# One more FFN piece at the mixer boundary, and a new schedule of weight casts, in a decoder layer on eight cores

## The chip, the cores and the metric

The kernel runs one decoder layer on 8 cores of one Trainium2 chip. The metric is device time in microseconds (us) of the slowest core. Cores 0 to 3 are one die, 4 to 7 the other.

Two programs share the work. The *first program* (cores 0 and 4) takes the first 4608 tokens of each of the two sequences: nine tiles of 512, of which the first two are worked as a pair. The *halo program* (cores 1, 2, 3, 5, 6, 7) takes 3928 tokens. Because its attention looks back 2048 tokens, it first works four tiles of halo in two pairs (the *pair stage*, roughly the first 680 us) and then eight own tiles.

Runs come in two states. In the slow state the cores of a die are granted a lower TensorE clock, and the time is longer by some per cent to 20%. Even among fast runs there is a step: in some of them cores 2 and 3 alone are granted 0.989 instead of about 0.998 and take some 30 us more.

## The reference, cut to what matters

```python
h = x + 0.5 * post1(SwiGLU1(pre1(x)))          # FFN1, 1024 -> 2816 -> 1024
u = pre_mix(h)                                 # then q/k/v projections, three attentions, a gated merge
h = h + post_mix(merged @ w_out)
y = h + 0.5 * post2(SwiGLU2(pre2(h)))          # FFN2
# pre*, post*, pre_mix, post_mix are RMS norms; 32768 tokens in all, D_MODEL 1024, D_FF 2816
```

The kernel's matmuls take bf16 weights, while the inputs are float32, so each core casts weights as it goes.

## The kernel before: the parts that matter

**Pieces.** The first half of an FFN (`x @ w_in`, SwiGLU) is cut into 22 pieces of 16 matmuls, one piece of weights each. While one tile is in its attention and its boundaries, pieces of the *next* tile's FFN1 are slipped in by `fill(1)`, so that TensorE has something to do:

```python
def fill(n):                     # F[0] is the generator of the next tile's FFN1 pieces
    for _ in range(n):
        if F[0] is None: return
        try: next(F[0])
        except StopIteration: F[0] = None
```

**Boundaries.** Between FFN1 and the mixer, and between the mixer and FFN2, a tile of 512 tokens is normalised and transposed block by block. TensorE transposes into PSUM; VectorE evicts into `xn`, times the gain (1.22 us for 128x1024 on core 2); only then can the next matmuls read `xn`. The end of this is `tail`. `gain` is 1 (G_MIX) at the mixer boundary, 2 (G_F2) before FFN2. The pair edges of the pair stage inherit `tail` with gain 1.

```python
def tail(self, more=lambda: fill(1)):
    fin_pool[0] = FIN4
    z = self.nb - 1
    more()
    self.scaled(z - 1)           # ScalarE: h * rstd of the last block but one
    self.stat(z)
    more()
    self.scaled(z)
    self.turn(z - 1)             # TensorE transposes, VectorE evicts to xn
    self.turn(z)
    more()
```

The order of each engine is fixed at build time by a list scheduler.

**Weights.** Eleven slots in SBUF hold weight pieces. A piece comes into a slot in one of two ways: by a cast from the float32 input (`wslot<-wf`, issued on POOL), or by a plain load from a bf16 copy in HBM (`wslot<-wsc`, issued on SP). The copy is made in one of two ways: by a *store* of a slot after some use (`wsc<-wslot`), or by an *ahead cast* in HBM, before any use (`wsc<-wf`):

```python
def release(k):                  # after a use of a piece
    ...
    if nm not in W["stored"] and n == stored_at(role, nm) and n + 1 < uses[nm]:
        W["stored"].add(nm)
        dma("sp", wsc[...], slots[s]..., ...)      # store: bf16 slot -> copy
def w_ahead(nm, gate=()):
    ...
    dma("pool", wsc[...], wf[...], ...)            # ahead cast: float32 -> bf16 copy
```

In the halo program before, the ahead casts are issued in the second half of the pair stage, one every two FFN pieces; the FFN2 pieces that are not cast ahead are stored at their first use (even numbers) or their second (odd ones):

```python
SECOND = ["f2_i%d" % f for f in range(9, NF, 2)]                    # stored at second use
LATE = [n for n in PT if n.startswith("f2_o")] + ["f2_i%d" % f for f in range(8)]   # 20 pieces
...
            while F[0] is not None:
                fill(1)
                step(prep)                 # row loads and squares of the next tile
                n += 1
                if n % 2 == 0 and late:
                    w_ahead(late.pop(0))
```

The softmax here doesn't subtract the row's maximum and nothing guards it: scores larger than these inputs give would overflow.

## Time and profile before

Six runs: 3479.99, 3509.78, 3511.83, 3695.24, 3801.16 and 3926.94 us, median 3603.54. The last three are slow. The profiled run was fast, with cores from 3465.0 to 3479.3 us at a granted clock of 0.996 to 0.998. Core 2 was the slowest.

The page of core 2, parts 1 and 4 (busy us per engine with the share of the span; then the chain of work that ended last, by engine):

```profile
PE 3430.2 (99%) x19230; PEld 1743.1 (50%) x19230; DVE 1690.0 (49%) x2656; ACT 955.8 (27%) x1685; POOL 853.0 (25%) x1161
...
PE 96%; DMA 2%; DVE 1%; ACT 1%; issue 1%; POOL 0%; SPq 0%; POOLq 0%; ACTq 0%; DVEq 0%
```

TensorE is the bound. What a change of order can win is TensorE's idle time, and the list of waits gives it. Its main lines for core 2 (what waited, for what: us in total, times, longest us):

```profile
PE ps L586 <- DMA wslot<-wsc: 9.0, 3, 4.0
PE ps L586 <- DVE xn L621: 6.7, 7, 1.6
PE ps L1582 <- DVE ident_sb L618: 5.8, 1, 5.8
PE ps L774 <- DVE q L631: 4.9, 4, 2.1
...
PE ps L586 <- ACT V L616: 3.1, 2, 2.3
```

All lines together come to 41.6 us, 1.2% of the span. The first line is the wait for weights and the second the wait for an evicted `xn`; the next two belong to start-up.

The wait for weights is at 480 to 490 us in the pair stage, in the second half of FFN1. The view of windows on core 2 shows the DMA engines full before it (columns: window, its length, busy us of PE, PEld, DVE, ACT, POOL with instruction counts, granted clock, DMA share, GB/s):

```profile
400.00:440.00 40.00, 40.00 (x187) 18.13 (x186) 16.50 (x24) 6.66 (x12) 5.85 (x12) 1.00 0.99 160
440.00:470.00 30.00, 30.00 (x141) 13.58 (x140) 6.56 (x6) 0.00 (x0) 1.46 (x3) 1.00 1.02 196
470.00:480.00 10.00, 7.58 (x36) 3.33 (x35) 5.88 (x7) 1.85 (x5) 3.88 (x2) 1.00 0.99 168
480.00:490.00 10.00, 3.42 (x13) 1.00 (x11) 2.10 (x4) 3.28 (x12) 7.38 (x6) 0.79 0.86 240
490.00:500.00 10.00, 10.00 (x41) 4.21 (x40) 0.00 (x0) 0.00 (x0) 0.00 (x0) 0.87 0.06 25
```

TensorE is busy 3.42 of 10 us. Cores 3, 6 and 7 show 7.3 to 7.6 us of the same wait, cores 1 and 5 none.

The wait for `xn` is the mixer boundary. The timeline of core 2's TensorE at one of them (start us, us, engine line op out<-in, count, and in brackets the idle time before it and who ended it):

```profile
1815.54 2.54 PE L586 MATMUL ps<-xn,wslot 128*128 128x512 bf16 x11
1817.91 0.61 PE L774 MATMUL ps<-ident_sb,mix 128*128 128x128 bf16 x8
1818.36 1.24 PE L586 MATMUL ps<-xn,wslot 128*128 128x512 bf16 x5
1820.31 1.89 PE L586 MATMUL ps<-xn,wslot 128*128 128x512 bf16 x8 [0.71 <-DVE xn L621]
```

The last transposes end, five matmuls of an FFN piece are left, and then the projections wait 0.71 us for the eviction. The boundary before FFN2 of the same core has no such wait, because there 20 matmuls of FFN1 pieces stand between the last transposes and FFN2 (the last line runs from them into FFN2 without a break):

```profile
2024.16 2.75 PE L586 MATMUL ps<-xn,wslot 128*128 128x512 bf16 x12
2026.75 0.61 PE L774 MATMUL ps<-ident_sb,mix 128*128 128x128 bf16 x8
2027.20 18.08 PE L586 MATMUL ps<-xn,wslot 128*128 128x512 bf16 x83
```

### The profile page before, as it was taken

To read this page: it belongs to the slowest core of one execution; us is meant where nothing else is said; L and a number is where in the kernel's file an instruction comes from. 1 tells how busy PE (TensorE), PEld (TensorE's weight loads), DVE (VectorE), ACT (ScalarE), POOL (GpSimd) and SP (SyncE) were. 2 spreads that over 40 slices of the span, in tenths; PEclk is the share of its full clock that TensorE was granted. 3 is DMA by queue.
4 is the path that set the end of the run, shared out by engine and by line. 5 is a ranking of instruction groups with operands and counts; after the bars stand their busy time and mean duration, and the time that the engine had idled before them with its cause. 6 is when DMAs were issued, how large, how long until landed. Compare 5 with 4: busy or idle time off the path is not lost.

```text
span 3479.3 us, 54875 instructions; the slowest of 8 cores (3465.0 to 3479.3 us)
## 1 busy us (share of the span) xinstructions
PE 3430.2 (99%) x19230; PEld 1743.1 (50%) x19230; DVE 1690.0 (49%) x2656; ACT 955.8 (27%) x1685; POOL 853.0 (25%) x1161
## 2 busy tenths in 40 slices
PE   8999989999999999999999999999999999999999
PEld 4445445454445544554445444554455444646555
DVE  4444334573437444564347343744456433736533
ACT  2223222232313331233122231333123312333321
POOL 3143122233214230413023211412040302323020
PEclk9999999999999999999999999999999999999999
DMA  9979967657878786668564456445463556446456
GB/s 205 200 159 219 169 127 242 151 129 156 186 238 217 135 213 189 226 151 239 171 221 131 148 177 211 159 131 181 153 222 124 168 161 218 149 150 216 144 170 207
DMA packets 177859, 623.20 MB, mean 179 GB/s; under 512 B 20288, under 2 KB 20928, under 8 KB 177584
## 3 DMA queue, kind: packets, MB, share of 16 engines
q1 hardware_dynamic: 128384, 452.09, 40.4%
q0 software_dynamic: 49200, 167.52, 25.4%
q8 instruction: 163, 2.67, 0.3%
q14 instruction: 112, 0.92, 0.1%
HBM read 659.13 MB, written 69.75 MB: 209 GB/s over the span
## 4 chain that ended last, share of the span: by engine, by line
PE 96%; DMA 2%; DVE 1%; ACT 1%; issue 1%; POOL 0%; SPq 0%; POOLq 0%; ACTq 0%; DVEq 0%
PE ps L586 94%; DMA wslot<-wsc 1%; PE ps L774 1%; DMA wslot<-wf 1%; PE ps L1265 1%; ACT mix L609 0%; DVE xn L621 0%; DMA h<-xh 0%; DVE mix L621 0%; POOL rstd L621 0%; DVE tsig L626 0%; DVE mix L995 0%; ACT tsig L609 0%; ACT q L609 0%; POOL rstd L631 0%
## 5 line engine op out<-in xcount | busy, mean ns | idle before, releaser
L586 PE MATMUL ps<-xn,wslot 128*128 128x512 bf16 (+3 forms) x9840 | 2139.4, 370 | 11.8 <-DVE xn L621 6.7
L586 PEld LDWEIGHTS ps<-xn,wslot 128*128 128x128 bf16 x9840 | 947.6, 98 | 1012.4 <-issue 21.2
L626 DVE SCALAR_TENSOR_TENSOR tsig<-tsig,ps 128x512 f32<-128x512 f32 (+1 forms) x418 | 279.1, 668 | 561.2 <-ACT tsig L609 558.9
L609 ACT ACTIVATE tsig<-ps 128x512 f32<-128x512 f32 (+1 forms) x418 | 242.8, 581 | 847.8 <-PE ps L586 846.5
L586 PE MATMUL ps<-wslot,hid 128*128 128x512 bf16 (+1 forms) x1892 | 413.3, 379 | 0.0
L586 PE MATMUL ps<-wslot,mix 128*128 128x512 bf16 (+1 forms) x1540 | 338.5, 381 | 9.0 <-DMA wslot<-wsc 9.0
L609 ACT ACTIVATE mix<-ps 128x512 bf16<-128x512 f32 (+4 forms) x334 | 210.1, 664 | 447.0 <-PE ps L586 446.0
L621 DVE TENSOR_TENSOR ps<-ps,gpost_sb 128x1024 f32<-128x1024 f32 (+1 forms) x110 | 125.7, 1144 | 401.9 <-ACT mix L609 225.2
L586 PEld LDWEIGHTS ps<-wslot,hid 128*128 128x128 bf16 (+1 forms) x1892 | 185.7, 98 | 220.7 <-issue 0.2
L626 DVE SCALAR_TENSOR_TENSOR mix<-mix,ps 128x512 f32<-128x512 f32 (+1 forms) x192 | 127.9, 666 | 321.8 <-PE ps L586 320.6
L621 POOL TENSOR_TENSOR q<-mix 128x512 bf16<-128x512 f32 (+1 forms) x144 | 216.5, 1504 | 187.2 <-DVE mix L995 115.3
L586 PEld LDWEIGHTS ps<-wslot,mix 128*128 128x128 bf16 (+1 forms) x1540 | 151.5, 99 | 191.4 <-issue 13.6
L609 ACT ACTIVATE mix<-ps,bgate_sb 128x512 f32<-128x512 f32 (+1 forms) x192 | 128.6, 670 | 331.1 <-PE ps L586 331.1
L995 DVE TENSOR_TENSOR mix<-ps,cst 64x512 f32<-64x512 f32 (+1 forms) x308 | 205.7, 668 | 20.6 <-DVE mix L995 0.9
L621 POOL TENSOR_TENSOR mix<-mix 128x512 f32<-128x512 f32 (+1 forms) x64 | 78.0, 1218 | 514.6 <-DVE mix L626 514.6
L621 DVE TENSOR_TENSOR hid<-tsig,ps 128x512 bf16<-128x512 f32 (+1 forms) x242 | 162.1, 670 | 85.0 <-PE ps L586 76.3
L641 POOL DMA_DIRECT2D wslot<-wf x144 | 79.9, 555 | 473.6 <-PE ps L586 291.9
L586 PE MATMUL ps<-mix,wslot 128*128 128x512 bf16 (+1 forms) x640 | 163.9, 370 | 0.0
L586 PE MATMUL ps<-wslot,xn 128*128 128x256 bf16 (+1 forms) x1200 | 155.1, 274 | 3.8 <-ACT V L616 2.3
L621 DVE TENSOR_TENSOR mix<-tsig,ps 128x512 bf16<-128x512 f32 (+1 forms) x176 | 117.2, 666 | 82.5 <-PE ps L586 80.8
L631 POOL TENSOR_SCALAR rstd<-ssq 128x1 f32<-128x1 f32 x178 | 42.1, 236 | 442.6 <-ACT mix L609 246.4
L586 PEld LDWEIGHTS ps<-wslot,xn 128*128 128x128 bf16 (+1 forms) x1200 | 126.5, 110 | 39.1 <-issue 5.4
(159 smaller groups left out, 2424.5 us busy)
## 6 DMA issues: line engine op xcount, KB each, us to landing
wslot<-wsc SPq DMA_DIRECT2D x688, 512.0 KB, 4.8
wslot<-wf POOLq DMA_DIRECT2D x118, 512.0 KB, 10.4
wsc<-wslot SPq DMA_DIRECT2D x71, 512.0 KB, 10.7
wslot<-wsc SPq DMA_DIRECT2D x40, 576.0 KB, 3.7
xs<-xh POOLq DMA_DIRECT2D x41, 512.0 KB, 7.5
h<-xh POOLq DMA_DIRECT2D x32, 512.0 KB, 9.5
y<-h POOLq DMA_DIRECT2D x28, 512.0 KB, 8.1
wslot<-wf POOLq DMA_DIRECT2D x24, 576.0 KB, 7.0
```

Of the source, the lines that this page charges most:

```text
L586: P.add("pe", lambda e: e.matmul(outV.ap, lhsT=lhsV.ap, rhs=rhsV.ap, start=start, stop=stop, skip_group_check=True), reads=[lhsV, rhsV], w ...
L609: return e.activation(out=outV.ap, in_=inV.ap, func=func, scale=scale.ap if isinstance(scale, View) else scale, **kw)
L621: P.add(eng, lambda e: e.tensor_tensor(out=outV.ap, in0=aV.ap, in1=bV.ap, op=op), reads=[aV, bV], writes=[outV], us=0.567 if op == ALU.pow ...
L626: P.add("dve", lambda e: e.scalar_tensor_tensor(out=outV.ap, in0=aV.ap, scalar=sc, in1=bV.ap, op0=op0, op1=op1), reads=[aV, bV] + ([scalar ...
L631: P.add(eng, lambda e: e.tensor_scalar(out=outV.ap, in0=aV.ap, scalar1=sc, scalar2=None, op0=op0), reads=[aV] + ([s1] if isinstance(s1, Vi ...
L641: P.add(eng, lambda e: e.dma_start(out=out, in_=in_), reads=reads, writes=writes, dma_key=key, nbytes=n)
L774: P.add("pe", lambda e, src=src, o_=o_: e.transpose(out=o_.ap, in_=src.ap, identity=ident.ap), reads=[src, ident.v(0, 128)], writes=[o_], ...
L995: P.add("dve", lambda e, a=a, z=z: e.tensor_tensor(out=t2.ap[a:a + 64, :], in0=p_.ap[z:z + 64, :], in1=cst.ap[z:z + 64, TT:TT + n], op=ALU ...
L1265: P.add("pe", lambda e, src=src, o_=o_: e.transpose(out=o_.ap, in_=src.ap, identity=ident.ap[0:n, 0:n]), reads=[src, ident.v(0, 128)], wri ...
```

## The change

The intent, in its author's words: "Same 18 casts, one every three steps; one more piece of the next tile's FFN between FFN1's last transposes and the mixer's projections."

```diff
+TAIL = {1: 2, 2: 1}
 def stored_at(role, nm):
+    if role and nm in THIRD:
+        return 2
     if nm in HELD[role] or role and nm in SECOND:
         return 1
-SECOND = ["f2_i%d" % f for f in range(9, NF, 2)]
+SECOND = ["f2_i%d" % f for f in range(6, NF, 2)]
+THIRD = ["f2_i%d" % f for f in range(7, NF, 2)]
-LATE = [n for n in PT if n.startswith("f2_o")] + ["f2_i%d" % f for f in range(8)]
+LATE_EVERY, LATE_FROM = 3, 31
+LATE = [n for n in PT if n.startswith("f2_o")] + ["f2_i%d" % f for f in range(6)]
 ...                                     # end of Boundary.tail
-                more()
+                for _ in range(TAIL[self.gain]):
+                    more()
 ...                                     # halo program, pair stage
+            def fill_late(k):
+                for _ in range(k):
+                    fill(1)
+                    n[0] += 1
+                    if n[0] >= LATE_FROM and n[0] % LATE_EVERY == 0 and late:
+                        w_ahead(late.pop(0))
-                n += 1
-                if n % 2 == 0 and late:
-                    w_ahead(late.pop(0))
```

So there are three changes in one: an extra piece at every boundary with gain 1; another number and pace of ahead casts; and stores of FFN2 pieces put off by one use. The order of the built programs corrects the words. Before, 20 LATE casts are issued in the pair stage; after, only 14, since the steps end before the list does. Direct casts into slots rise by 23 in the halo program (118 to 141 of 512 KB on core 2) and not at all in the first (213 on core 4). At the first of the two pair edges the extra step is four pieces, since `tail` is called there with `fill(4)`.

More of the change, by code (lines that the diff above doesn't have):

```diff
@@ L1626, in trace @@
             memory_prep()
-            fill(6)
+            n = [0]
+            def fill_late(k):
[4 more added lines that the diff above has]
+                        w_ahead(late.pop(0))
+            fill_late(6)
             memory_turn(xn2)
             for _ in memory(xn2):
-                fill(6)
+                fill_late(6)
             prep = prep_iter(4)
-            n = 0
             while F[0] is not None:
-                fill(1)
+                fill_late(1)
                 step(prep)
-                n += 1
-                if n % 2 == 0 and late:
-                    w_ahead(late.pop(0))
             drain(prep)
```

## The prediction

> **What bounds it now.** TensorE: PE is busy 3430 of 3479 us (99%, profile page) and is 96% of the chain of waits. The list of waits gives core 2's TensorE about 42 us of idle time, so removing waits can win 1.2% at most:
> - Weights in the halo cores' pair stage, 480 to 490 us: 9.0 us on core 2, 7 to 8 on cores 3, 6, 7, none on 1 and 5. The DMA row is full from 280 to 475 us; the 20 ahead-of-use casts there take 28 us each to land (view of DMA issues).
> - Mixer boundary: the projections wait for the eviction of the last transposes (xn by DVE, 1.22 us): 6.7 us in 7 waits on core 2, 7.6 to 7.9 on cores 0 and 4.
> - Start-up, about 18 us: untouched.
> - Pair stage at 268 to 272 and 543 us: 2.4 and 2.3 us.
>
> **What the change does.** The matmul work is equal.
>
> 1. One FFN piece (16 matmuls, 3.45 us) moves to the mixer boundary. In the built order the matmuls between last transposes and projections go from 12 or 13 to 28 or 29, which covers the eviction: -6 to -8 us per core. But a tile has 22 pieces. Before, the 22nd covered the same eviction before FFN2: the run after the last FFN2-boundary transposes falls from 372 to 356, of which 352 are FFN2 itself, so cover drops from 20 matmuls (4.3 us) to 4 (0.86 us). In the timeline those transposes end at 2027.2 us, the eviction runs 2027.47 to 2028.69, FFN2 could start about 2028.9, and PE would run dry at 2028.1. A new wait of about 0.85 us in 5 or 6 tiles: +4 to +5 us. Net -1 to -3 us: the wait moves rather than vanishes.
>
> 2. Casts. The words say "same 18"; in the built order I count 14 ahead casts in the halo program's pair stage instead of 20. Six fewer transfers of 1 MB read and 0.5 MB written in the saturated stretch should remove the 7 to 9 us weight wait on cores 2, 3, 6, 7. The cost comes later: 23 more direct casts, mostly in FFN2 of the first own tiles, 20 in a row in the first (now 14), 16 in the second (now 7), where the DMA row is already at 1.0. Core 4 runs 22 per FFN2 with almost no cast waits, so I expect 0 to 5 us. [...]
>
> 3. The pair edge gets one more step: part of the 2.3 and 2.4 us may go.
>
> **Prediction.** Cores 2, 3, 6, 7: -5 to -12 us; the others -3 to +2. The slowest core ends near 3472 us in a fast profile (3479 before). Three of six runs before were slow (to 3927), fast ones 3480 to 3512; a median over mixed runs can lie far higher, so my figure is 3485 us, range 3455 to 3610. Faster by over 2%: 2%; within 2%: 96%; slower: 2%.
>
> **Right or wrong shows as.** Projections' waits for xn gone, 5 or 6 new ones before FFN2; the weight wait near 480 us gone; ahead casts landing under 28 us; waits for direct casts at 900 to 980 and 1280 to 1350 us under 5 us.
>
> **What would make it wrong.** Direct casts starving FFN2 in the first own tiles (10 us or more); another share of slow runs.

## The result, and the profile after

A ratio is the mean time of one kernel's fast runs over that of the other's fast runs of the same rounds, so it is not quite the ratio of the medians quoted. It is 0.9976, 95% interval 0.9953 to 0.9999: the same within 2%, faster by about a quarter of a per cent. The medians over all runs, slow ones included, were 3476.49 us after (20 runs) and 3509.0 us before (now 40 runs). The low fast times of before lie at 3479 to 3484 us, those of after at 3473 to 3477 us.

In the profiled run (fast) the spans of cores 0 to 7 are 3473.1, 3461.2, 3463.3, 3462.1, 3473.4, 3466.9, 3464.5 and 3461.4 us. The halo cores gained; cores 0 and 4 did not (3470.5 and 3472.3 before) and are now the slowest. The page of core 4, parts 1 and 4, looks like that of before and tells nothing of this:

```profile
PE 3413.2 (98%) x18896; PEld 1697.9 (49%) x18896; DVE 1662.0 (48%) x2608; ACT 956.2 (28%) x1636; POOL 881.5 (25%) x1164
...
PE 96%; DVE 1%; issue 1%; ACT 1%; DMA 1%; POOL 0%; DVEq 0%; ACTq 0%; POOLq 0%; SPq 0%
```

The list of waits of core 2 does (the lines of the kernel are shifted by 7 or 8; L593 is the old L586, L628 the old L621):

```profile
PE ps L1590 <- issue: 6.8, 1, 6.8
PE ps L593 <- DVE xn L628: 6.7, 8, 1.2
PE ps L781 <- DVE q L638: 4.7, 4, 2.1
PE ps L593 <- ACT V L623: 3.6, 2, 2.7
...
PE ps L593 <- DMA wslot<-wsc: 0.2, 1, 0.2
```

The wait for weights is gone, 9.0 to 0.2 us. The wait for `xn` has not moved at all in its sum: 6.7 us before, 6.7 us after. The windows of core 2 show the DMA engines done before the weights are needed, and no fall of the clock:

```profile
400.00:440.00 40.00, 40.00 (x187) 18.08 (x185) 15.89 (x24) 6.57 (x11) 3.70 (x7) 1.00 1.00 173
440.00:470.00 30.00, 30.00 (x140) 13.59 (x139) 8.79 (x8) 0.00 (x0) 0.00 (x0) 1.00 0.71 195
470.00:480.00 10.00, 10.00 (x48) 4.53 (x47) 4.88 (x8) 5.02 (x16) 5.02 (x5) 1.00 0.33 107
480.00:490.00 10.00, 10.00 (x48) 4.56 (x47) 4.04 (x6) 3.09 (x7) 7.33 (x10) 1.00 0.00 0
490.00:500.00 10.00, 10.00 (x60) 5.01 (x58) 6.33 (x8) 6.11 (x11) 3.30 (x8) 1.00 0.00 1
```

The timeline of core 2 shows where the `xn` wait went. At the mixer boundary 29 matmuls now follow the last transposes without a break: the five of before, the 16 of the extra piece and the first eight of the projections. Nothing waits:

```profile
1802.60 2.54 PE L593 MATMUL ps<-xn,wslot 128*128 128x512 bf16 x11
1805.10 0.61 PE L781 MATMUL ps<-ident_sb,mix 128*128 128x128 bf16 x8
1805.54 6.42 PE L593 MATMUL ps<-xn,wslot 128*128 128x512 bf16 x29
1811.80 0.38 PE L593 MATMUL ps<-wslot,xn 128*128 128x256 bf16 x2
```

Before FFN2 only four are left, and FFN2 waits 0.73 us:

```profile
2014.51 2.75 PE L593 MATMUL ps<-xn,wslot 128*128 128x512 bf16 x12
2017.10 0.61 PE L781 MATMUL ps<-ident_sb,mix 128*128 128x128 bf16 x8
2017.55 1.03 PE L593 MATMUL ps<-xn,wslot 128*128 128x512 bf16 x4
2019.30 26.06 PE L593 MATMUL ps<-xn,wslot 128*128 128x512 bf16 x120 [0.73 <-DVE xn L628]
```

### The profile page after: what moved, and what is told of

The parts are those of the page before. It is cut to its first block, busy times and chain, and to the rows that moved or that the text cites. A ratio compares the mean times of both kernels' runs of the same rounds, so it can differ in the third digit from the quotient of the medians.

```text
span 3473.4 us, 53905 instructions; the slowest of 8 cores (3461.2 to 3473.4 us)
## 1 busy us (share of the span) xinstructions
PE 3413.2 (98%) x18896; PEld 1697.9 (49%) x18896; DVE 1662.0 (48%) x2608; ACT 956.2 (28%) x1636; POOL 881.5 (25%) x1164
## 4 chain that ended last, share of the span: by engine, by line
PE 96%; DVE 1%; issue 1%; ACT 1%; DMA 1%; POOL 0%; DVEq 0%; ACTq 0%; POOLq 0%; SPq 0%
PE ps L593 94%; PE ps L781 1%; ACT mix L616 1%; PE ps L1273 1%; DMA wslot<-wsc 1%; DVE mix L628 0%; DVE xn L628 0%; DVE mix L1003 0%; DVE tsig L633 0%; DMA wslot<-wf 0%; PE ps L1590 0%; POOL rstd L628 0%; DVEq L361 0%; ACT q L616 0%; DVE ps L628 0%
## 5 line engine op out<-in xcount | busy, mean ns | idle before, releaser
L593 PE MATMUL ps<-xn,wslot 128*128 128x512 bf16 (+1 forms) x9776 | 2198.5, 377 | 12.0 <-DVE xn L628 6.6
L593 PEld LDWEIGHTS ps<-xn,wslot 128*128 128x128 bf16 x9776 | 942.0, 98 | 1078.7 <-issue 27.1
L633 DVE SCALAR_TENSOR_TENSOR tsig<-tsig,ps 128x512 f32<-128x512 f32 x374 | 256.8, 687 | 550.1 <-ACT tsig L616 549.1
L616 ACT ACTIVATE tsig<-ps 128x512 f32<-128x512 f32 x374 | 222.9, 596 | 829.4 <-PE ps L593 829.4
L616 ACT ACTIVATE mix<-ps 128x512 bf16<-128x512 f32 (+1 forms) x356 | 228.2, 676 | 496.2 <-PE ps L593 491.8
L593 PE MATMUL ps<-wslot,mix 128*128 128x512 bf16 x1584 | 348.1, 380 | 2.6 <-DMA wslot<-wsc 2.6
L593 PE MATMUL ps<-wslot,hid 128*128 128x512 bf16 x1584 | 345.3, 379 | 0.0
L628 DVE TENSOR_TENSOR ps<-ps,gpost_sb 128x1024 f32<-128x1024 f32 (+1 forms) x109 | 128.6, 1182 | 438.1 <-ACT mix L616 253.7
L628 POOL TENSOR_TENSOR q<-mix 128x512 bf16<-128x512 f32 x162 | 252.5, 1560 | 225.1 <-DVE mix L1003 141.4
L628 POOL TENSOR_TENSOR mix<-mix 128x512 f32<-128x512 f32 x72 | 90.9, 1263 | 632.2 <-DVE mix L633 632.2
L593 PEld LDWEIGHTS ps<-wslot,mix 128*128 128x128 bf16 x1584 | 154.9, 98 | 188.9 <-issue 6.0
L593 PEld LDWEIGHTS ps<-wslot,hid 128*128 128x128 bf16 x1584 | 154.7, 98 | 186.0 <-issue 0.7
L1003 DVE TENSOR_TENSOR mix<-ps,cst 64x512 f32<-64x512 f32 x324 | 223.1, 689 | 21.7 <-DVE mix L1003 0.9
L593 PE MATMUL ps<-mix,wslot 128*128 128x512 bf16 x720 | 190.7, 379 | 0.0
L628 DVE TENSOR_TENSOR hid<-tsig,ps 128x512 bf16<-128x512 f32 x198 | 135.6, 685 | 69.2 <-PE ps L593 63.1
L593 PE MATMUL ps<-wslot,xn 128*128 128x256 bf16 x1184 | 154.7, 275 | 3.4 <-DVE hid L633 2.4
L628 DVE TENSOR_TENSOR mix<-tsig,ps 128x512 bf16<-128x512 f32 x176 | 120.9, 687 | 73.1 <-PE ps L593 69.6
L593 PEld LDWEIGHTS ps<-wslot,xn 128*128 128x128 bf16 x1184 | 123.2, 106 | 41.7 <-issue 5.0
```

The source lines that it names most:

```text
L593: P.add("pe", lambda e: e.matmul(outV.ap, lhsT=lhsV.ap, rhs=rhsV.ap, start=start, stop=stop, skip_group_check=True), reads=[lhsV, rhsV], w ...
L616: return e.activation(out=outV.ap, in_=inV.ap, func=func, scale=scale.ap if isinstance(scale, View) else scale, **kw)
L628: P.add(eng, lambda e: e.tensor_tensor(out=outV.ap, in0=aV.ap, in1=bV.ap, op=op), reads=[aV, bV], writes=[outV], us=0.567 if op == ALU.pow ...
L633: P.add("dve", lambda e: e.scalar_tensor_tensor(out=outV.ap, in0=aV.ap, scalar=sc, in1=bV.ap, op0=op0, op1=op1), reads=[aV, bV] + ([scalar ...
L1003: P.add("dve", lambda e, a=a, z=z: e.tensor_tensor(out=t2.ap[a:a + 64, :], in0=p_.ap[z:z + 64, :], in1=cst.ap[z:z + 64, TT:TT + n], op=ALU ...
```

## The experiments

All kernels gave correct results. The table collects the median span of each core over the fast runs, in us. The runs were made on three chips, each time with the kernel before beside them. That kernel's own medians on cores 2, 3, 6 and 7 differ by up to 5.5 us, so between rows of the table only larger differences count. Because the chip times mix in the step of cores 2 and 3, I judge by these spans and by the traces.

| kernel | fast runs | cores 0, 4 | cores 1, 5 | cores 2, 3, 6, 7 |
|---|---|---|---|---|
| before | 5 | 3472.9, 3474.8 | 3464.9, 3462.5 | 3476.9, 3473.5, 3475.9, 3477.3 |
| after (first result) | 18 | 3472.9, 3473.0 | 3461.2, 3461.9 | 3465.3, 3462.0, 3464.1, 3462.6 |
| after_again | 3 | 3474.2, 3469.3 | 3462.5, 3463.2 | 3464.6, 3463.2, 3462.6, 3464.3 |
| casts_only | 6 | 3473.1, 3474.2 | 3470.6, 3471.1 | 3475.8, 3469.8, 3473.7, 3473.1 |
| piece_only | 4 | 3473.6, 3470.5 | 3464.1, 3461.9 | 3478.1, 3478.1, 3477.0, 3475.5 |
| both_covered | 5 | 3471.3, 3470.7 | 3454.5, 3453.2 | 3458.3, 3455.5, 3456.4, 3456.0 |
| pair_edge_only | 5 | 3475.4, 3474.9 | 3463.5, 3463.8 | 3463.7, 3462.6, 3466.1, 3463.9 |
| tiles_only | 2 | 3474.1, 3471.9 | 3469.3, 3470.7 | 3473.5, 3468.1, 3473.4, 3470.9 |
| both_tiles | 4 | 3470.3, 3471.2 | 3454.7, 3455.1 | 3457.4, 3454.8, 3457.9, 3453.9 |
| casts14_every2 | 5 | 3473.1, 3471.7 | 3459.9, 3462.8 | 3463.1, 3463.2, 3462.9, 3463.4 |
| casts_prep_later | 4 | 3473.1, 3472.2 | 3467.4, 3467.4 | 3486.3, 3483.0, 3468.2, 3471.4 |
| early20 | 4 | 3473.6, 3474.4 | 3461.4, 3460.9 | 3471.1, 3466.8, 3472.0, 3472.7 |
| fewer_old_pace | 3 | 3473.8, 3472.6 | 3471.1, 3472.7 | 3484.5, 3478.5, 3484.3, 3483.7 |
| both_tiles_4600 | 4 | 3464.2, 3465.9 | 3457.9, 3453.9 | 3457.5, 3454.8, 3456.2, 3455.2 |
| casts_prep_latest | 4 | 3472.1, 3476.1 | 3463.8, 3461.3 | 3462.9, 3462.1, 3463.9, 3461.7 |
| stores_as_before | 6 | 3472.3, 3474.9 | 3464.6, 3463.8 | 3473.9, 3468.7, 3474.1, 3473.4 |

### The yardstick: the changed kernel again

> The changed kernel once more, as the yardstick of this chip. Both theories: ratio 0.998 to the kernel before; slowest core near 3474 us and of the first program (cores 0 and 4); cores 2, 3, 6, 7 at 3461 to 3466 us.

It repeated: ratio 0.9988, interval 0.9966 to 1.0009, from only three fast runs at 3475.8 to 3476.1 us. Halo cores and first program stood where they were.

### The two halves apart

casts_only is the changed kernel with the extra piece taken out (its 14 casts become 15, since the pair stage has more steps left):

```diff
-TAIL = {1: 2, 2: 1}
+TAIL = {1: 1, 2: 1}
```

> The changed casts, without the extra piece at the mixer boundary. Theory A (the casts give the whole gain, the piece only moves a wait): cores 2, 3, 6, 7 fall from 3468-3479 to 3461-3468 us, the weight wait near 480 us is under 1 us, cores 0 and 4 stay at 3470-3474 us, projections still wait about 7 us for xn; chip time within 2 us of the changed kernel. Theory B (the piece gives the gain): under 3 us of gain on the halo cores, chip time near 3480 us.

The wait for weights near 480 us was gone on all halo cores, as theory A has it. But the halo cores came to 3470 to 3476 us, not to 3461 to 3468, and cores 1 and 5 even lost 6 to 9 us. Theory A failed here: the casts alone do not give the gain. The timeline of core 2 shows a new wait, at a pair edge near 550 us:

```profile
551.16 3.57 PE L593 MATMUL ps<-xn,wslot 128*128 128x512 bf16 x8 [3.67 <-DVE xn L628]
```

After the wait of 3.67 us these 8 matmuls took 3.57 us, where 8 take 1.89 us elsewhere, so the gap costs once more after it has ended (the granted clock was 0.68 between 550 and 560 us). All six halo cores have such a wait here, 3.5 to 5.5 us, also cores 1 and 5, which had no wait for weights to lose; in the kernel before none has it.

piece_only is the kernel before with the extra piece:

```diff
-                more()
+                for _ in range(TAIL[self.gain]):
+                    more()          # TAIL = {1: 2, 2: 1}
```

> The extra piece alone, with the old casts. Theory A: TensorE's total wait for xn is unchanged within 1.5 us (6.7 us on core 2), but stands before FFN2 instead of before the projections; cores 0 and 4 within 2 us of before; cores 2, 3, 6, 7 keep 5 us or more of weight wait near 480 us, chip time 3475 to 3481 us. Theory B: the xn wait falls below 2 us and every core gains 5 us or more.

As theory A: the weight wait stayed (8.8 us on core 2 between 470 and 495 us), cores 2, 3, 6 and 7 did not gain (3475.5 to 3478.1 us), and cores 0 and 4 moved by +0.7 and -4.3 us, within what they move between runs of one kernel. The wait for `xn` on core 2, from the list of waits:

```profile
PE ps L588 <- DMA wslot<-wsc: 9.1, 4, 3.7
PE ps L588 <- DVE xn L623: 6.7, 9, 1.2
```

6.7 us once more. So neither half alone gives the 12 us of the changed kernel on cores 2, 3, 6 and 7. The two act together.

### Where they act together: the pair edges

The extra piece goes to two kinds of place: the pair edges of the pair stage, and the mixer boundaries of the later tiles. pair_edge_only and tiles_only keep the changed casts and give it to one kind each:

```diff
-                for _ in range(TAIL[self.gain]):
+                for _ in range(2 if isinstance(self, PairEdge) else 1):                 # pair_edge_only
+                for _ in range(1 if isinstance(self, PairEdge) else TAIL[self.gain]):   # tiles_only
```

> The changed casts, with the extra step only at the pair edges of the first stage, none at the mixer boundaries of later tiles. Theory A2 (the casts give the gain of the halo cores only together with the extra step at the pair edge, which keeps TensorE fed while ScalarE stands before a late row load; the extra pieces of the later tiles only move a wait): cores 1, 2, 3, 5, 6, 7 at 3461 to 3467 us, no wait of 2 us or more for xn near 550 us, projections still waiting 0.7 to 1.6 us per tile. Rival B2 (the pieces of the later tiles are what halo cores gained over the casts alone): halo cores stay at 3469 to 3476 us. Both: cores 0 and 4 at 3469 to 3475 us.

> The changed casts, with the extra piece only at the mixer boundaries of later tiles, none at the pair edges. Theory A2: like the casts alone, halo cores 3469 to 3476 us with a wait of about 3.7 us for xn near 550 us on core 2. Rival B2: halo cores at 3461 to 3467 us.

Theory A2 holds on both. With the piece at the pair edges alone the halo cores are at 3462.6 to 3466.1 us, as in the changed kernel; with it in the later tiles alone they are at 3468.1 to 3473.5 us, as with the casts alone (only two fast runs, so no ratio, but the trace agrees: core 2 waits 5.46 us for `xn` at 551.79 us). The extra pieces in the later tiles, which the change's words put first, give nothing. (The ratio of pair_edge_only is 0.9985, interval 0.9971 to 0.9998.)

Why does the pair edge need it? In casts_only TensorE reaches this edge some 10 us sooner (its last transposes start at 542.98 us on core 2, against 553.98 us in the kernel before), and there the loads of the next tile's rows (`xs<-xh`) are under way with everything else: the DMA share was 0.96 to 1.00 between 530 and 550 us. In casts_only ScalarE stands 6.76 us at a square of those rows, with two of the FFN's activations (`tsig`) behind it in its list, and runs these only after the square, from 546.48 us (timeline of core 2's ScalarE):

```profile
538.06 0.60 ACT L616 ACTIVATE tsig<-ps 128x512 f32<-128x512 f32 x1 [2.91 <-PE ps L593]
545.42 1.06 ACT L616 ACTIVATE q<-xs 128x1024 bf16<-128x1024 f32 x1 [6.76 <-DMA xs<-xh]
...
546.48 1.06 ACT L616 ACTIVATE tsig<-ps 128x512 f32<-128x512 f32 x2
```

In the trace VectorE then does the late `tsig` and only after it the eviction to `xn` (548.56 us) that TensorE waits for. To test this, casts_prep_later and casts_prep_latest leave the edge without an extra piece and only start the row loads later after the second pair edge:

```diff
                 prep = prep_iter(i + 1)
+                fill(5)                  # casts_prep_later; fill(10) in casts_prep_latest
                 while F[0] is not None:
                     fill(1)
                     step(prep)
+                    step(prep)           # casts_prep_latest only
```

> The changed casts without any extra piece; only the next tile's row loads and their squares begin five FFN pieces later after the second pair edge. Theory A2 (what keeps the casts alone from giving the gain is that ScalarE, in order, stands before a row load that DMA has not landed, and the activations behind it hold up the eviction that TensorE waits for): the wait of 3.7 us for xn near 550 us on core 2 falls under 1 us, halo cores go from 3469-3476 to 3464-3469 us. If instead the extra FFN work at the edge itself is needed: the wait stays at 3 us or more and the halo cores stay at 3469-3476 us.

This was inconclusive. Cores 1, 5, 6 and 7 gained 1.7 to 5.5 us on casts_only, less than expected on most; cores 2 and 3 stood in their low-clock step in two of the four fast runs and say nothing. In the trace core 6 had 0.56 us of `xn` wait near 540 us, but core 7 still 1.98 us for `xn` and 2.46 us for `tsig`, and core 2, of which under 1 us was expected, 1.86 us for `xn`. The reason to go on was that one square still stood behind a single activation.

> As casts_prep_later, with the row loads ten FFN pieces later, so that the first square that waits for a row load stands behind three activations of the FFN instead of one. If a row load in front of the FFN's activations is what eats the casts' gain: on cores 2, 3, 5, 6, 7 less than 1.5 us of waits for xn and tsig between 530 and 570 us, halo cores 3462 to 3467 us in the undisturbed runs. If delay of the loads does not matter beyond what casts_prep_later gave: 3467 to 3471 us.

This one settled it. The halo cores are at 3461.3 to 3463.9 us without any extra piece, like the changed kernel. (With a ratio of 0.9966, interval 0.987 to 1.0061, the chip time alone says nothing.) It has 15 ahead casts, as casts_only has, so it was not the one cast more that held casts_only back. It also changes only what follows the second pair edge, so the first one did not hold it back either. On core 2 there is only one wait of this kind left, 0.46 us for `tsig` at 563 us. ScalarE's list has three activations in front of the first square, and the row has nearly landed when it gets there:

```profile
540.26 0.60 ACT L616 ACTIVATE tsig<-ps 128x512 f32<-128x512 f32 x1 [3.75 <-PE ps L593]
541.47 1.06 ACT L616 ACTIVATE q<-xs 128x1024 bf16<-128x1024 f32 x1 [0.61 <-DMA xs<-xh]
```

In the changed kernel the square waits as well, but two activations stand in front of it, not one, and TensorE has 40 matmuls, the last eight of them projections, to do after the transposes (core 2):

```profile
537.17 0.60 ACT L616 ACTIVATE tsig<-ps 128x512 f32<-128x512 f32 x1 [1.22 <-PE ps L593]
541.65 1.06 ACT L616 ACTIVATE q<-xs 128x1024 bf16<-128x1024 f32 x1 [3.89 <-DMA xs<-xh]
539.53 8.80 PE L593 MATMUL ps<-xn,wslot 128*128 128x512 bf16 x40
```

So the extra piece gives TensorE work at the pair edge and shifts the order of ScalarE's list. Moving the loads does the second alone, and that is enough.

### Number of casts or pace of casts

casts14_every2 is the changed kernel with the same 14 casts at the old pace; early20 has all 20 at the new pace, beginning earlier:

```diff
-LATE_EVERY, LATE_FROM = 3, 31
+LATE_EVERY, LATE_FROM = 2, 31      # casts14_every2, with LATE cut to f2_o and f2_i0, f2_i1
+LATE_EVERY, LATE_FROM = 3, 13      # early20, with LATE to f2_i7
```

> The changed kernel with the same 14 casts ahead, but one every two steps as before, not every three. If the number of casts is what ended the weight wait near 480 us: wait under 1 us, halo cores within 2 us of the changed kernel. If the slower pace is what ended it: 5 us or more of the wait return on cores 2, 3, 6, 7 and they stand at 3466 us or more.

> The changed kernel with 20 casts ahead, one every three steps, but from step 15 on instead of 33. If the number of casts before the DMA queue has to be empty is what counts: the weight wait near 480 us is back at 3 us or more on some of cores 2, 3, 6, 7, since the last cast is issued at the same step as in the changed kernel and the stretch was full before. If only the pace counts: no wait.

At the old pace with 14 casts there is no wait for weights on any halo core in this stretch, and the halo cores are at 3459.9 to 3463.4 us (ratio 0.9981, interval 0.9967 to 0.9995). With 20 casts at the new pace the wait is back, 4.2, 3.6, 7.9 and 9.8 us on cores 2, 3, 6 and 7. The line of core 7:

```profile
PE ps L593 <- DMA wslot<-wsc: 9.8, 3, 3.9
```

The number counts. The pace was hardly put to the test, because the casts did not come out at it: on core 2 the ahead casts of the changed kernel were issued from 315.3 to 412.9 us and those of casts14_every2 from 315.5 to 414.5, with POOL waiting for earlier ahead casts to land (30.8 and 36.7 us in all). With 20 casts the last was issued at 451.0 us before and still at 448.6 us in early20, which began at 291.7 us. The stretch was full before the first cast (in the kernel before, the DMA share of core 2 was 1.00 between 270 and 290 us, with the first cast at 308.6 us), and with the earlier start the last cast was issued only 2.4 us earlier.

### What six fewer ahead casts cost later

fewer_old_pace is the kernel before with nothing but a shorter list:

```diff
-LATE = [...] + ["f2_i%d" % f for f in range(8)]
+LATE = [...] + ["f2_i%d" % f for f in range(2)]
```

> The kernel before with nothing changed but the list of ahead casts cut from 20 to 14 (the other six are cast at their first use). If the number of casts causes the weight wait: wait near 480 us under 1 us on cores 2, 3, 6, 7; by A2 the halo cores gain only part of it, 3466 to 3476 us, as in the run with the changed casts alone.

The wait near 480 us was gone, but the kernel became slower: ratio 1.0025, interval 1.0006 to 1.0044, halo cores at 3471 to 3485 us, where I had expected 3466 to 3476. Part of this is the wait for `xn` at the second pair edge, as in casts_only: 1.3 to 5.7 us on the halo cores. On cores 1 and 5 it is the larger part, 5.7 and 5.4 us, against 1.0 and 2.2 us of waits for loads later. The later cost came where I had looked for it in the prediction, in FFN2 of the first own tile, but not in direct casts: in weight *loads*. On core 6, waits between 900 and 1060 us:

```profile
PE ps L586 <- DMA wslot<-wsc: 12.0, 2, 9.4
```

Neither the kernel before nor the changed one has any wait for DMA there. The changed one differs in that its stores are put off. stores_as_before is the changed kernel with the old rule for the stores:

```diff
-SECOND = ["f2_i%d" % f for f in range(6, NF, 2)]
-THIRD = ["f2_i%d" % f for f in range(7, NF, 2)]
+SECOND = ["f2_i%d" % f for f in range(9, NF, 2)]
+THIRD = []
```

> The changed kernel, but the FFN2 pieces are stored as before (even ones and the six no longer cast ahead at first use, odd ones from 9 on at second use). If the put-off stores are what kept the later cost of the change small: 5 us or more of weight waits between 900 and 1000 us, as in fewer_old_pace (12 us on core 6), halo cores 3468 to 3478 us. If they do not matter: waits under 1 us there and halo cores at 3461 to 3466 us.

The waits are back, 5.5, 4.8, 5.2 and 3.6 us on cores 2, 3, 6 and 7 in the same window, and these cores stand at 3468.7 to 3474.1 us, nearly where they were before the change. On core 2:

```profile
PE ps L593 <- DMA wslot<-wsc: 5.5, 2, 3.1
```

The waits of SP, which issues loads and stores from one list, fit this: on core 6 between 880 and 1060 us it stood 21.8 us for stores in fewer_old_pace and 15.8 us in stores_as_before, with 13 and 12 stores issued there; in the kernel before and in the changed one it stood for none, with ten and four. So putting off the stores is a needed third part: it keeps the stores out of the tile that has just received the casts.

### Giving both boundaries a spare piece

If the piece only moves a wait because a tile has 22 pieces and both boundaries want a spare one, a piece from elsewhere should end both waits. both_covered takes the one between the two heads of mixer A; both_tiles does so except in the two paired tiles of cores 0 and 4:

```diff
-TAIL = {1: 2, 2: 1}
+TAIL = {1: 2, 2: 2}
             attn_a(i, 0, 4)
-            fill(1)
+            if paired:               # both_tiles; no fill at all in both_covered
+                fill(1)
             attn_a(i, 1, 4)
```

> The changed kernel, with the piece taken from between the two heads of mixer A, so that both the mixer boundary and the FFN2 boundary have one left over. Theory A (a tile has 22 pieces and both boundaries need a spare): the xn wait falls from about 6.7 to under 2.5 us on every core, unless the attention opens a new wait of the same size where the piece was; cores 0 and 4 near 3469 us, chip time 3468 to 3472 us. Theory C (the xn wait is not a matter of spare pieces): xn wait stays at 5 us or more and the time stays at 3474-3477 us.

The wait for `xn` fell from 6.7 to 1.4 us on core 2 and from 6.6 to 2.6 us on core 4, and the attention opened no new wait of that size. The halo cores ended 6.5 to 9 us earlier than in the changed kernel. The chip gained less than I had expected of cores 0 and 4: these lost part of it in their paired tiles, where waits of 3.31 us (2.44 before) and a new one of 1.52 us appeared on core 4 at 556 and 602 us. Ratio 0.9979, interval 0.9963 to 0.9995.

> As the run both_covered, but in the first two (paired) tiles of cores 0 and 4 the piece between the heads stays where it was, since those tiles have no mixer boundary to cover and lost about 2.4 us there. Expected if a spare at both boundaries is what is missing: xn waits under 2.5 us, halo cores at 3453 to 3459 us as before, cores 0 and 4 at 3467 to 3471 us, chip time 3468 to 3472 us, 1 to 2 us below both_covered. If start-up noise of cores 0 and 4 decides instead: no change against 3472 to 3474 us.

Those two waits are as before the change again. Ratio 0.9969, interval 0.9954 to 0.9984, cores 0 and 4 at 3470.3 and 3471.2 us. On core 4 no wait for `xn` is left after 700 us (4.1 us in the changed kernel), but the same core waited 6.9 us for weights there in this run against 2.6 us in the changed kernel's. So cores 0 and 4 gained about 2 us by the medians, which is less than core 4 of the kernel before moves (6 us), and end at the upper edge of what I expected. Whether the wait for weights is set by the order or is noise I did not test.

### The bound of the chip time

Cores 0 and 4 are the slowest in the changed kernel. Sixteen tokens too many are handed out over both sequences (4608 + 3 x 3928 = 16392, for 16384 each). both_tiles_4600 takes the eight of each sequence from the first program:

```diff
-FIRST = 4608
+FIRST = 4600
-    yd = nc.dram_tensor("y", [FIRST, D], ...)
+    yd = nc.dram_tensor("y", [-(-FIRST // 128) * 128, D], ...)
```

> As both_tiles, and the first program takes 4600 tokens instead of 4608 (the eight doubly computed tokens dropped), since its cores 0 and 4 are now the slowest. Its last tile is 504 wide instead of 512, 1.6% of about 250 us of matmuls with the tokens as moving side: cores 0 and 4 lose 3 to 5 us, to 3465-3468 us, the others unchanged at 3453-3461 us, chip time 3466 to 3470 us. If cores 0 and 4 do not bound the chip time, it stays at 3472 us.

The 3 to 5 us, and the 250 us in them, were an estimate; in the trace of the changed kernel the 128x512 matmuls of core 4 that read `xn` are busy for 236.4 us between 3100 and 3480 us. That their time goes with their width is near what the kernel before shows on core 2: its 8608 of 128x512 are busy for 1959.5 us, 0.228 us each, and its 1040 of 128x344 for 163.9 us, 0.158 us each.

Cores 0 and 4 fell by 5 to 6 us on both_tiles, the others stayed within 3.2 us of it, and the chip time fell with cores 0 and 4: fast runs at 3466.95 to 3469.4 us, against 3469.9 to 3473.1 us of both_tiles. Ratio 0.9967, interval 0.9952 to 0.9983. But against the kernel before beside them their ratios are nearly equal (0.9969 and 0.9967), so how much of the 5 to 6 us the tokens gave is not shown. This version beats the kernel before: its fast runs lie some 12 us under the low fast runs of that kernel. They also lie 6 to 8 us under those of the changed kernel. They were run at other times.

## Why the prediction was right or wrong

**The figure: wrong.** The line says 3485 us, beside 3603.54 us for the kernel before. Read as a change, that is 3485 / 3603.54 = 0.967, a gain of 3.3%, and the measured one is 0.24%. The argument of the text gave something else: 7 us of 3479, or 0.2%, "near 3472 us in a fast profile", and the fast profile shows 3473.4 us. The step that failed is "a median over mixed runs can lie far higher, so my figure is 3485 us". The baseline of 3603.54 us was a median of three fast and three slow runs, midway between 3511.83 and 3695.24; with 40 runs it is 3509.0. I carried an allowance for slow runs into my figure and set it against a baseline that held another share of them. Of the 20 runs after, only three were slow, so their median, 3476.49, is a fast run's time. The figure to record was the baseline times the ratio argued for fast runs, with the state left to the range.

**The extra piece moves a wait: right.** Predicted was a new wait of about 0.85 us before FFN2 in 5 or 6 tiles; it is 0.72 to 1.05 us in six tiles on core 2. The net of -1 to -3 us was too hopeful: the sum on core 2 is 6.7 us before and after, and piece_only does not move cores 0 and 4 beyond noise. Six of the seven old waits went (5.1 us), the one in the last tile only shrank (1.58 to 1.15 us), and the six new ones come to 5.3 us. The prediction's counts of 12 or 13 and 28 or 29 matmuls before the projections include the first eight of the projections themselves; the real cover was five and became 21.

**The wait for weights goes with six fewer casts: right**, and shown by casts14_every2 and early20. That 14 casts are issued, not 18, was read from the order of the built program. The landing time barely moved, 28.2 to 26.8 us; what changed on core 2 is that the last ahead cast was issued at 412.9 instead of 451.0 us, so that the DMA share was down to 0.33 at 470 to 480 us.

**The later cost, "0 to 5 us": right in size, wrong in its reason.** I argued from core 4, which makes 22 casts per FFN2 almost without waits (0.3 us for `wslot<-wf` over the whole run before). The cost is not in casts but in loads that stand behind stores (SP stood 21.8 us for stores in fewer_old_pace, 15.8 us in stores_as_before), and it is small because the change puts the stores off: 3.6 to 5.5 us return in stores_as_before, up to 12 us in fewer_old_pace. The prediction did not look at the stores.

**The pair edge: mis-sized.** "Part of the 2.3 and 2.4 us may go" was the smallest term of the sum, and it decides whether the casts' gain is kept at all: without the extra step (casts_only) the halo cores end 8 to 10.5 us later than with it. The cause is shown by casts_prep_latest. The wait that was removed brought TensorE some 10 us sooner to the next place where DMA was behind (share 0.96 to 1.00 there), and I had treated the terms as if they added up. I had also not counted the clock: on core 2, waits between 260 and 680 us fell from 15.3 to 5.3 us, but the distance between the same two transposes, at 261.79 and 680.42 us before and 259.63 and 665.97 after, fell by 12.3 us, with 2044 matmuls in both (TensorE busy 403.51 us at a granted clock of 0.99 before, 401.16 us at 1.00 after).

**Cores: nearly right.** Cores 0, 1, 4 and 5 were to move by -3 to +2 us; by medians cores 0 and 4 moved by 0 and -1.8 us, 1 and 5 by -3.7 and -0.6. Cores 2, 3, 6 and 7 were to gain 5 to 12 us and gained 11.5 to 14.7 us by the medians of the table. The chip gained only what the slowest group left it, since cores 0 and 4 do not run this pair stage.

## What to carry to other kernels

A spare piece of work is a fixed stock: before moving one to cover a wait, count what it covers now. When a wait is taken away, follow the engine to the next place it will now reach too early, and look at what stands in front in the lists of the other engines, as the square stood 6.76 us in front of two activations here. And with several programs on one chip, name the core that will be the slowest afterwards, since the gain ends there.

## What the runs and traces showed of the clock and of DMA

- All eight cores ran matmuls for 98 to 99% of their span of about 3.47 ms (profiled runs before and after), at a granted clock of 0.994 to 0.999 in the fast runs, but for the few that had it lowered on some cores. Slow runs of the changed kernel had different values on one die (0.812 to 0.817 at 4167 us, 0.930 to 0.938 at 3689 us).
- A lower clock did not always take the whole die. In some runs cores 2 and 3 alone were at 0.989, some 30 us longer, while cores 0 and 1 of the same die stood at 0.996 and above.
- Matmuls after a wait were sometimes slow, and the length of the wait alone does not tell when. In casts_only on core 2, 8 matmuls took 3.57 us after a wait of 3.67 us, where 8 take 1.89 us, and at 533 us 8 took 1.87 us after one of 2.68 us, where 8 take 1.04 us. In the kernel before, on core 2, 8 took 1.76 us instead of 1.04 us at 543 us after a wait of 2.27 us, but at 479 us, after one of 2.42 us, 8 took their 1.89 us. On core 2 the stretch of the pair stage quoted above became 12.3 us shorter where its waits became 10.0 us shorter, so a list of waits undercounted by about 2 us what such gaps cost here.
- Casts and loads kept the same 16 DMA engines busy: between 250 and 500 us of the kernel before, on core 2, POOL's queue with its casts took 59.0% of the 16 engines' time and SP's 33.0%. In the full stretch an ahead cast from HBM to HBM, 512 KB of bf16, landed after 26.8 us (after) and 28.2 us (before), by the medians of core 2.
